# Gate and up products of four feed-forward chunks by seven block products in place of eight, with the weight sums on GpSimd

## The chip, the core and the metric

The kernel runs on one core of one Trainium2 chip. A core has TensorE (PE in the profile) for matrix products, VectorE (DVE), ScalarE (ACT) and GpSimd (POOL) for elementwise work, and SyncE (SP), which here only issues DMAs. Each engine works through its own queue in order and waits on semaphores for the others. Products go to PSUM (eight banks of 128x512 fp32); everything else lies in SBUF. The metric is the device time of one execution in microseconds, the median of three runs.

## The reference

A two-layer network on 256 positions of width 1024, in float32. Each layer is a feed-forward block, a mixer (latent attention and a gated recurrence in layer 0, differential attention in layer 1) and a second feed-forward block, each with a norm before and after and a residual. What matters here is the feed-forward block, which runs four times with weights 1024x2816, 1024x2816 and 2816x1024:

```python
def swiglu(x, w_gate, w_up, w_down):
    return (jax.nn.silu(x @ w_gate) * (x @ w_up)) @ w_down

h = swiglu(rms_norm(x, g[0, 0]), ffn_w_gate[l, 0], ffn_w_up[l, 0], ffn_w_down[l, 0])
x = x + 0.5 * rms_norm(h, g[0, 1])
```

## The kernel before

**Precision.** A product of float32 operands is made of three products of rounded ones: each operand is held as `hi` (rounded to float32r) and `lo` (the rest), and `mm3` adds hi·hi, hi·lo and lo·hi. One k tile of 128 rows and 512 columns is therefore three matmuls. The moving operand is the weight, the stationary one a 128x128 tile of the turned activations.

**Weights.** All weights lie in HBM in one array `w` in the order of use. `emit_load` loads a subunit of [128, 1024] on SP's queue into one of five `raw` buffers (pool `wraw`), ScalarE rounds it (`whi`, line 219), and VectorE subtracts (`wlo`, line 224: SBUF raw less SBUF hi). The pair goes to `queue`; `fill` keeps seven subunits ahead of TensorE. An order on VectorE is forced for all `wlo` (`after`); all other instructions are ordered by a scheduler by their priority, and `high_priority` marks those of norms and turned operands. The `hi` and `lo` of a feed-forward block go to its own pool of `BUFS_F` = 7 pairs, those of other parts to `wsp` with five.

**A feed-forward block.** The 256 positions are two tiles t of 128. The 2816 hidden columns are cut into six chunks, `CHUNKS` = 512, 512, 256, 512, 512, 512. For each chunk `group` makes the gate product of both tiles (`pg`), `silu` reads it, the previous chunk's h is transposed (`turn`, line 353 on TensorE, then a rounding and a split, lines 360 and 361), `group` makes the up product (`pu`), `gated` multiplies (line 445), and `down` adds the previous chunk's part to the four banks y. So each weight subunit is used for both tiles: a gate subunit of two k tiles feeds 2 x 2 x 3 = 12 matmuls, and a down subunit as many. The last two chunks' down products come at the end; there `finish` makes the norm, the residual and the turned operand of the next block, half by half, between the last products. The first chunk is made by `group_first`, tile 0 ahead of tile 1, while tile 1's operand `xT[1]` is still being turned.

**Names.** `xT[t]` is the turned input of a block, (hi, lo), eight k tiles; `hT[t]` the turned h of a chunk; `oT` the turned output of a mixer, free in a feed-forward block. GpSimd makes little: the power -0.5 of each norm (lines 343 and 388), and some elementwise work in the mixers (lines 708, 709, 791, 1007).

Of the kernel before, what the change touches and what calls it, by code (L numbers as in the profile page):

```python
# [12 lines left out]
F32 = mybir.dt.float32  # L13
# [21 lines left out]
BUFS_F = 7  # L35
CHUNKS = [512, 512, 256, 512, 512, 512]

# ---------------------------------------------------------------- weight stream
# A unit is (name, index, first k tile, k tiles, column ranges): [128, k tiles, columns],
# stored contiguously in the order of use.  # L40


def _ffn_units(l, j):
# [12 lines left out]
    for ci, (a, w) in enumerate(starts):  # L56
        step = 2048 // w
        for k in range(0, KD, step):
# [54 lines left out]
for _i in range(1, len(UNITS)):  # L113
    if UNITS[_i - 1][0].endswith("w_out") and not UNITS[_i][0].endswith("w_out"):
# [8 lines left out]
def _pack(inputs):  # L123
    parts = []
    for name, idx, k0, nk, cols in UNITS:
# [6 lines left out]
# ---------------------------------------------------------------- constants of the shapes  # L132
# [37 lines left out]
def forward(ctx, tc, a):  # L170
# [19 lines left out]
    # ------------------------------------------------------------ weight stream  # L190
    SPLIT = 1024
    state = {"i": 0, "off": 0, "block": -1, "pool": None, "first": None, "n": 0}
# [3 lines left out]

    def emit_load():
        if state["i"] >= len(UNITS):
            return
        u = UNITS[state["i"]]  # L200
        pool, tag = (state["pool"], "f") if BLOCK_OF[state["i"]] == state["block"] else (wsp, "w")
# [3 lines left out]
        off = state["off"]  # L205
        state["off"] += P * width
        src = a["w"][off:off + P * width].rearrange("(p n) -> p n", p=P)
        nc_ = width // nk
        per = max(1, SPLIT // nc_)
        for k in range(0, nk, per):  # L210
            n = min(per, nk - k)
            w = n * nc_
            raw = wraw.tile([P, SPLIT], F32, name="raw", tag="raw")
            moved = nc.sync.dma_start(raw[:, :w], src[:, k * nc_:k * nc_ + w])
            if state["n"] in late:
                after(late[state["n"]](), moved)
# [13 lines left out]
    def take(nk):  # L230
        """The next subunits that make up nk k tiles."""
# [31 lines left out]
    def group(pss, lhss, n, nk=KD, k0=0):  # L263
        """pss[t][:, :n] = lhs_t^T @ the next weight group [nk*128, n]; a step of side work after each subunit."""
# [46 lines left out]
    # ------------------------------------------------------------ start  # L311
# [19 lines left out]
    def after(b, a_):  # L331
        """b is issued after a_ (on one engine)."""
# [5 lines left out]
    def rpow(ss, n, mul, add):  # L338
        """(ss * mul + add) ** -0.5"""
# [6 lines left out]
    def to_T(src, dst, n, j0=0, bank=bank):  # L346
        """dst[(hi, lo)][:, j0:j0+n, :] = transposes of the n 128-column blocks of src."""
# [15 lines left out]
    def turn_x(t, xg):  # L363
        """Closures: halves of xT[t] = xg^T, split."""
# [11 lines left out]
    def post_norm(t, ys, g, half, gnext):  # L376
        """x[t] += (0.5 if half) rms(y) g; returns xg = x[t] * gnext."""
# [40 lines left out]
    # ------------------------------------------------------------ FFN  # L418
# [750 lines left out]
```

## Time and profile before

| | |
|---|---|
| Median of three runs | 1028.74 us (1028.34 to 1030.66) |
| Profiled execution, its own span | 1027.8 us |
| TensorE busy | 1011.3 us (98%), 4979 matmuls seen |
| VectorE busy | 625.8 us (61%) |
| ScalarE busy | 517.1 us (50%) |
| GpSimd busy | 49.9 us (5%) |
| HBM read | 182.35 MB, 178 GB/s over the span |

The four feed-forward blocks begin at about 11, 343, 531 and 843 us of the span; the mixers lie from 200 to 340 and from 720 to 840. The profile comes from one execution. Busy times count an instruction from its start to its modelled end; on TensorE instructions overlap, so the distance from one start to the next tells what one costs, not its length.

### The profile page before, as it was taken

What the parts mean: (1) busy time and instruction counts of PE and PEld (TensorE: products, weight loads), DVE (VectorE), ACT (ScalarE), POOL (GpSimd) and SP (SyncE); (2) the same over time, 40 slices, a digit from 0 to 9 for tenths busy, and PEclk for the clock granted to TensorE, in tenths of its full rate; (3) what the DMA queues carried; (4) which work ended last, traced back from release to release, by engine and by line L of the source; (5) the groups of instructions that cost most, each with busy time, mean ns of one, the idle gap of its engine ahead of it and who ended that gap; (6) DMA issues with size and microseconds to landing.
All of it is one profiled execution on the core that took longest, in us unless ns stands there. A gap on an engine that the chain in (4) does not pass through costs nothing.

```text
span 1027.8 us, 13158 instructions
## 1 busy us (share of the span) xinstructions
PE 1011.3 (98%) x4979; PEld 843.5 (82%) x4979; DVE 625.8 (61%) x876; ACT 517.1 (50%) x757; POOL 49.9 (5%) x61
## 2 busy tenths in 40 slices
PE   8999999999999999999999999999999999999997
PEld 6888888888788889888888888888877878888886
DVE  6555585768577855455576555546676786455553
ACT  6544455477644644444554444444665565444441
POOL 1000000021201000000000000000011200000000
PEclk8999999999999999999999999999999999999999
DMA  8765555575221765555547555555634366655531
GB/s 282 271 202 186 186 184 189 180 225 194 86 81 58 253 212 196 185 184 187 182 164 246 187 183 189 191 190 168 208 121 147 102 206 225 201 182 189 186 123 41
DMA packets 51903, 184.25 MB, mean 179 GB/s; under 512 B 6136, under 2 KB 6528, under 8 KB 51840
## 3 DMA queue, kind: packets, MB, share of 16 engines
q1 hardware_dynamic: 48960, 176.05, 51.8%
q10 hardware_dynamic: 2880, 7.37, 2.1%
q8 instruction: 39, 0.64, 0.2%
q14 instruction: 24, 0.20, 0.1%
HBM read 182.35 MB, written 1.05 MB: 178 GB/s over the span
## 4 chain that ended last, share of the span: by engine, by line
PE 90%; DVE 4%; issue 3%; ACT 1%; DMA 1%; POOL 1%; SPq 0%; DVEq 0%; POOLq 0%; ACTq 0%
PE w L244 16%; PE w L246 16%; PE w L245 16%; PE y L246 9%; PE y L244 9%; PE y L245 9%; PE w L292 7%; PE w L353 2%; DVE wlo L224 1%; PE y L353 1%; DMA raw<-in_w_dram 1%; ACT whi L219 1%; POOL pm L1007 0%; DVE E L857 0%; DVE pm L1009 0%
## 5 line engine op out<-in xcount | busy, mean ns | idle before, releaser
L224 DVE TENSOR_TENSOR wlo<-raw,whi 128x1024 fp32r<-128x1024 f32 (+2 forms) x331 | 404.0, 1227 | 283.6 <-ACT whi L219 281.2
L219 ACT CAST whi<-raw 128x1024 fp32r<-128x1024 f32 (+1 forms) x331 | 345.0, 1049 | 365.5 <-PE w L246 206.6
L244 PE MATMUL w<-whi,xThi 128*128 128x512 f32 (+1 forms) x836 | 315.6, 377 | 0.0
L246 PE MATMUL w<-whi,xTlo 128*128 128x512 f32 (+1 forms) x836 | 312.0, 373 | 0.0
L245 PE MATMUL w<-wlo,xThi 128*128 128x512 f32 (+1 forms) x836 | 311.5, 373 | 0.0
L246 PEld LDWEIGHTS w<-whi,xTlo 128*128 128x128 f32 x836 | 157.3, 188 | 28.3 <-issue 0.3
L244 PEld LDWEIGHTS w<-whi,xThi 128*128 128x128 f32 x836 | 157.5, 188 | 27.5 <-issue 1.0
L245 PEld LDWEIGHTS w<-wlo,xThi 128*128 128x128 f32 x836 | 157.5, 188 | 26.4
L244 PE MATMUL y<-whi,hThi 128*128 128x512 f32 x352 | 138.4, 393 | 0.0
L246 PE MATMUL y<-whi,hTlo 128*128 128x512 f32 x352 | 137.2, 390 | 0.0
L245 PE MATMUL y<-wlo,hThi 128*128 128x512 f32 x352 | 137.1, 389 | 0.0
L246 PEld LDWEIGHTS y<-whi,hTlo 128*128 128x128 f32 x352 | 66.1, 188 | 14.0
L245 PEld LDWEIGHTS y<-wlo,hThi 128*128 128x128 f32 x352 | 66.1, 188 | 13.2
L244 PEld LDWEIGHTS y<-whi,hThi 128*128 128x128 f32 x352 | 66.1, 188 | 13.2
L361 DVE TENSOR_TENSOR hTlo<-w,hThi 128x512 fp32r<-128x512 f32 (+1 forms) x48 | 29.1, 640 | 34.0 <-ACT hThi L360 34.0
L440 ACT ACTIVATE s<-w,sm 128x512 f32<-128x512 f32 (+1 forms) x48 | 31.4, 653 | 25.9 <-PE w L246 20.3
L388 POOL TENSOR_TENSOR sm<-sm,mhalf 128x1 f32<-128x1 f32 x12 | 6.6, 550 | 726.6 <-DVE sm L386 726.6
L292 PE MATMUL w<-whi,xThi 128*128 128x512 f32 (+2 forms) x124 | 39.1, 397 | 2.6 <-ACT xThi L360 2.6
L292 PE MATMUL w<-wlo,xThi 128*128 128x512 f32 (+2 forms) x124 | 37.8, 389 | 0.4 <-DVE wlo L224 0.4
L292 PE MATMUL w<-whi,xTlo 128*128 128x512 f32 (+2 forms) x124 | 37.9, 390 | 0.0
L445 DVE SCALAR_TENSOR_TENSOR h<-w,sm,s 128x512 f32<-128x512 f32 (+1 forms) x48 | 32.0, 699 | 0.7 <-PE w L246 0.5
L292 PEld LDWEIGHTS w<-whi,xThi 128*128 128x128 f32 x124 | 22.6, 192 | 6.6 <-ACT xThi L360 3.1
(246 smaller groups left out, 820.2 us busy)
## 6 DMA issues: line engine op xcount, KB each, us to landing
raw<-in_w_dram SPq DMA_DIRECT2D x325, 512.0 KB, 3.6
g<-in_norm_g_dram ACTq DMA_DIRECT2D x9, 512.0 KB, 4.6
raw<-in_w_dram SPq DMA_DIRECT2D x4, 448.0 KB, 3.4
g<-in_norm_g_dram SPq DMA_DIRECT2D x2, 512.0 KB, 6.2
out_dram<-x SPq DMA_DIRECT2D x4, 256.0 KB, 2.1
E<-in_hw_dram ACTq DMA_DIRECT2D x1, 576.0 KB, 6.7
x<-in_x_dram SPq DMA_DIRECT2D x2, 256.0 KB, 3.0
x<-in_x_dram SPq DMA_DIRECT2D x1, 512.0 KB
```

Source lines behind the costliest of these rows:

```text
L219: c = nc.scalar.copy(hi[:, :w], raw[:, :w])
L224: state["lo"] = nc.vector.tensor_tensor(lo[:, :w], raw[:, :w], hi[:, :w].bitcast(F32), op=ALU.subtract)
L244: mm(ps, hi[:, j, :], rhi, start=start, stop=False)
L245: mm(ps, hi[:, j, :], rlo, start=False, stop=False)
L246: state["mm"] = mm(ps, lo[:, j, :], rhi, start=False, stop=stop)
L292: state["mm"] = mm(o, lhs[:, k, :], rhs[:, i, :], start=j == 0 and k == 0, stop=j == 2 and k == KD - 1)
L353: nc.tensor.transpose(ps[:, i * P:(i + 1) * P], src[:, (b + i) * P:(b + i + 1) * P], ident)
L361: return c, nc.vector.tensor_tensor(lo.rearrange("p a b -> p (a b)"), ps, h2.bitcast(F32), op=ALU.subtract)
L388: nc.gpsimd.tensor_tensor(r, v, mhalf[:, :1], op=ALU.pow)
L440: nc.scalar.activation(s[:, :w], ps[:, :w], AF.Silu, scale=r[t])
L445: nc.vector.scalar_tensor_tensor(hh[:, :w], ps[:, :w], r[t], s[:, :w], op0=ALU.mult, op1=ALU.mult)
```

## The change

In the second, fourth, fifth and sixth chunk of each feed-forward block (`SEVEN` counts from 0) gate and up are seen as one product of 2x2 blocks: the rows are the two tiles of positions, the inner dimension is cut into two halves of four k tiles, and the columns are gate (B11 above, B21 below) and up (B12, B22). It is made by seven block products in the form of Strassen and Winograd. Each is [128 x 512] by [512 x 512], four k tiles of three matmuls, for one tile of positions' sum:

- X from A11·B11; W from S1·T1; X adds S2·T2; Y from A12·B21; X adds S3·T3; X adds A22·T4; W adds S4·B22. ScalarE copies X to SBUF three times on the way (`held`), VectorE adds a PSUM bank to a copy three times (`plus`), and `silu` and `gated` read the results.
- Row sums S1 to S4 (`row_sums`, once a block): GpSimd adds hi and lo of `xT`, makes four sums and four `lo`, twelve operations 128x512; ScalarE makes four `hi`. S1 and S2 lie in `oT`.
- Weight sums on GpSimd (`emit_load`), in two tiles of 1024 columns each: T1 = B12 - B11, T2 = B22 - T1, T3 = T2 - B11, T4 = B21 - T2, in place in the raw tiles. T1 to T4 and B11, B21, B22 are each rounded and split as a weight is: 14 subunits a chunk for 8.
- The raw tiles of these chunks come from a pool of eight (`raws`); the pairs of a block come from its own pool, now four, and from `wsp`, five, in turn (`RING`). Of the previous chunk's down products one half stands between T3 and T4, the other behind B22; in the sixth chunk all stand behind.

The core of the diff (comments that the diff removes are left out):

```diff
-BUFS_F = 7
+BUFS_F = 4
+SEVEN = (1,3,4,5)
+RAWS = 8
+RING = "wfwfwfwfw"
...
+        if ci in SEVEN:
+            gate, up = ([("ffn_w_" + n, (l, j), k, 4, [(a, a + w)]) for k in (0, 4)] for n in ("gate", "up"))
...
+            units += [gate[0] + ("B11",), up[0] + ("T1",), up[1] + ("T2",), gate[1] + ("B21",), (None, None, 0, 4, [(a, a + w)], "T3")]
+            units += d[:half] + [(None, None, 0, 4, [(a, a + w)], "T4"), (None, None, 0, 4, [(a, a + w)], "B22")] + d[half:]
+            continue
...
+                raw = (wraw if kind is None else state["raws"]).tile([P, SPLIT], F32, name="raw", tag="raw")
...
+                sub = nc.gpsimd.tensor_tensor
+                if kind in ("B11", "B21"):
+                    kept[kind, k] = raw
+                elif kind == "T1":
+                    sub(raw, raw, kept["B11", k], op=ALU.subtract)
+                    kept["T", k] = raw
+                elif kind == "T2":
+                    kept["B22", k] = raw
+                    sub(kept["T", k], raw, kept["T", k], op=ALU.subtract)
+                    raw = kept["T", k]
+                elif kind == "T3":
+                    raw = kept["B11", k]
+                    sub(raw, kept["T", k], raw, op=ALU.subtract)
+                elif kind == "T4":
+                    raw = kept["B21", k]
+                    sub(raw, raw, kept["T", k], op=ALU.subtract)
+                else:
+                    raw = kept["B22", k]
...
+            def row_sums(fp):
...
+                        tt(A[t][i], hi, lo, op=ALU.add)
+                tt(A[1][1], A[1][0], A[1][1], op=ALU.add)
+                tt(A[1][0], A[0][0], A[1][0], op=ALU.subtract)
+                tt(A[0][0], A[1][1], A[0][0], op=ALU.subtract)
+                tt(A[0][1], A[0][1], A[0][0], op=ALU.subtract)
...
+                    nc.scalar.copy(hi, v)
+                    tt(lo, v, hi.bitcast(F32), op=ALU.subtract)
...
+            def prod(ps, lhs, start):
...
+                        mm3(ps, lhs, k, hi[:, i, :], lo[:, i, :], start and k == 0, k == 3, not start)
...
+                X = bank()
+                prod(X, half(0, 0), True)
+                hT = [turn(0, CHUNKS[ci - 1]), None]
+                W = bank()
+                prod(W, S1, True)
+                p1 = held(X)
+                hT[1] = turn(1, CHUNKS[ci - 1])
+                prod(X, S2, False)
+                Y = bank()
+                prod(Y, half(0, 1), True)
+                u2 = held(X)
+                s0 = silu(0, plus(p1, Y), 512)
+                prod(X, S3, False)
+                downs(range(kf))
+                u3 = held(X)
+                c22 = plus(u3, W)
+                prod(X, half(1, 1), False)
+                s1 = silu(1, X, 512)
+                prod(W, S4, False)
+                h = [gated(0, plus(u2, W), s0, 512), gated(1, c22, s1, 512)]
+                downs(range(kf, wp))
...
+            sums = row_sums(fp)
             for ci in range(1, nch):
                 w, wp = CHUNKS[ci], CHUNKS[ci - 1]
+                if ci in SEVEN:
+                    seven(ci)
+                    continue
...
-    nc = _bacc.Bacc("TRN2", target_bir_lowering=False, num_devices=1)
+    nc = _bacc.Bacc("TRN2", target_bir_lowering=False, num_devices=1, dynamic_dma_scratch_size=512)
```

How this moves instructions, at three places. First VectorE at the start of the third feed-forward block, before: the last splits of the first chunk and of the second chunk's first weights, then the first chunk's h, then on with weights.

```order
L361 TENSOR_TENSOR xTlo1_94<-y_4749,xThi1_93 128x512
...
L224 TENSOR_TENSOR wlo_4803<-raw_4800,whi_4802 128x1024
L224 TENSOR_TENSOR wlo_4809<-raw_4806,whi_4808 128x1024
L445 SCALAR_TENSOR_TENSOR h_4840<-w_4672,sm_4631,s_4729 128x512
L445 SCALAR_TENSOR_TENSOR h_4842<-w_4673,sm_4652,s_4780 128x512
L224 TENSOR_TENSOR wlo_4849<-raw_4846,whi_4848 128x1024
```

The same place after. raw_4965 and raw_4971 are the halves of B11, raw_5010 and raw_5017 hold first T1 and then T2.

```order
L408 TENSOR_TENSOR xTlo1_94<-y_5030,xThi1_93 128x512
L271 TENSOR_TENSOR wlo_4810<-raw_4807,whi_4809 128x1024
L271 TENSOR_TENSOR wlo_4956<-raw_4953,whi_4955 128x1024
L271 TENSOR_TENSOR wlo_4962<-raw_4959,whi_4961 128x1024
L271 TENSOR_TENSOR wlo_4968<-raw_4965,whi_4967 128x1024
L271 TENSOR_TENSOR wlo_4974<-raw_4971,whi_4973 128x1024
L271 TENSOR_TENSOR wlo_5014<-raw_5010,whi_5013 128x1024
L271 TENSOR_TENSOR wlo_5021<-raw_5017,whi_5020 128x1024
L271 TENSOR_TENSOR wlo_5085<-raw_5010,whi_5084 128x1024
L271 TENSOR_TENSOR wlo_5092<-raw_5017,whi_5091 128x1024
L494 SCALAR_TENSOR_TENSOR h_5123<-w_4951,sm_4906,s_5008 128x512
```

Seven splits stand between the operand's last half and the splits of T2 (wlo_5085, wlo_5092), and h now stands behind these two.

Second, GpSimd at the same place, before: only the powers of the norms.

```order
L388 TENSOR_TENSOR sm_4569<-sm_4566,mhalf_87 128x1
L343 TENSOR_TENSOR sm_4631<-sm_4629,mhalf_87 128x1
L388 TENSOR_TENSOR sm_4640<-sm_4637,mhalf_87 128x1
L343 TENSOR_TENSOR sm_4652<-sm_4650,mhalf_87 128x1
```

And after, from the add of tile 1's second half on: xf are the sums, oTlo and Slo the four `lo`, then T2 and T3 of either half.

```order
L524 TENSOR_TENSOR xf_5128<-xThi1_93,xTlo1_94 128x512
L525 TENSOR_TENSOR xf_5128<-xf_5128 128x512
L526 TENSOR_TENSOR xf_5128<-xf_5127,xf_5128 128x512
L527 TENSOR_TENSOR xf_5127<-xf_5128,xf_5127 128x512
L528 TENSOR_TENSOR xf_5127<-xf_5127 128x512
L534 TENSOR_TENSOR oTlo0_96<-xf_5128,oThi0_95 128x512
...
L534 TENSOR_TENSOR Slo1_5140<-xf_5127,Shi1_5139 128x512
L249 TENSOR_TENSOR raw_5010<-raw_5081,raw_5010 128x1024
L253 TENSOR_TENSOR raw_4965<-raw_5010,raw_4965 128x1024
L249 TENSOR_TENSOR raw_5017<-raw_5088,raw_5017 128x1024
L253 TENSOR_TENSOR raw_4971<-raw_5017,raw_4971 128x1024
```

Nine operations stand ahead of T2's first half, and T3's first half stands ahead of T2's second. In the other three blocks T2's halves stand behind the second and the third `lo`.

Third, VectorE around the fifth chunk's h in the second block, before: four splits of 1024 columns since the turned h, then h.

```order
L361 TENSOR_TENSOR hTlo_4095<-w_4096,hThi_4094 128x512
L361 TENSOR_TENSOR hTlo_4104<-w_4105,hThi_4103 128x512
L224 TENSOR_TENSOR wlo_4117<-raw_4114,whi_4116 128x1024
L224 TENSOR_TENSOR wlo_4123<-raw_4120,whi_4122 128x1024
L224 TENSOR_TENSOR wlo_4153<-raw_4150,whi_4152 128x1024
L224 TENSOR_TENSOR wlo_4159<-raw_4156,whi_4158 128x1024
L445 SCALAR_TENSOR_TENSOR h_4186<-w_4112,sm_3141,s_4090 128x512
```

After, the last eight rows ahead of the fifth chunk's h: the sixth chunk's B11, T1 and T2 (raw_4418, raw_4424, raw_4444, raw_4451), with one `plus` (u) between.

```order
L271 TENSOR_TENSOR wlo_4421<-raw_4418,whi_4420 128x1024
L271 TENSOR_TENSOR wlo_4427<-raw_4424,whi_4426 128x1024
L271 TENSOR_TENSOR wlo_4448<-raw_4444,whi_4447 128x1024
L271 TENSOR_TENSOR wlo_4455<-raw_4451,whi_4454 128x1024
L271 TENSOR_TENSOR wlo_4479<-raw_4444,whi_4478 128x1024
L564 TENSOR_TENSOR u_4354<-w_4273,u_4354 128x512
L271 TENSOR_TENSOR wlo_4486<-raw_4451,whi_4485 128x1024
L494 SCALAR_TENSOR_TENSOR h_4471<-u_4354,sm_3282,s_4357 128x512
```

The next chunk's sums and their splits have moved ahead of this chunk's h.

## Rows read from the trace of the kernel before

**Rows 1.** The page: engine, busy us, share of the span, instructions.

```profile
PE 1011.3 (98%) x4979; PEld 843.5 (82%) x4979; DVE 625.8 (61%) x876; ACT 517.1 (50%) x757; POOL 49.9 (5%) x61
```

**Rows 2.** Waits: who waited for whom, total us, times, longest us.

```profile
DVE wlo L224 <- ACT whi L219: 281.2, 227, 2.8
ACT whi L219 <- PE w L246: 206.6, 131, 2.0
```

**Rows 3.** Timeline of TensorE: start us, us, engine, line, operation; twelve matmuls apart.

```profile
389.03 0.39 PE L244 MATMUL y<-whi,hThi 128*128 128x512 f32 x1
...
391.75 0.39 PE L244 MATMUL y<-whi,hThi 128*128 128x512 f32 x1
```

**Rows 4.** Groups by form on VectorE and ScalarE: busy us, mean ns; idle before.

```profile
L224 DVE TENSOR_TENSOR wlo<-raw,whi 128x1024 fp32r<-128x1024 f32 x325 | 398.3, 1231 | 283.6 <-ACT whi L219 281.2
L613 DVE RECIPROCAL lbm<-tmp 128x512 f32<-128x512 f32 x1 | 3.4, 3352 | 0.7 <-ACT tmp L612 0.7
L539 DVE SCALAR_TENSOR_TENSOR ang<-n,ang 128x80 f32<-128x80 f32 x12 | 2.9, 241 | 0.3
...
L219 ACT CAST whi<-raw 128x1024 fp32r<-128x1024 f32 x325 | 340.2, 1053 | 362.0 <-PE w L246 206.6 <-PE y L246 101.9 <-issue 24.5
```

**Rows 5.** Timeline of VectorE in the second feed-forward block.

```profile
407.31 1.22 DVE L224 TENSOR_TENSOR wlo<-raw,whi 128x1024 fp32r<-128x1024 f32 x1 [2.02 <-ACT whi L219]
408.45 1.28 DVE L361 TENSOR_TENSOR hTlo<-w,hThi 128x512 fp32r<-128x512 f32 x2
```

**Rows 6.** Groups by form on GpSimd.

```profile
L708 POOL TENSOR_TENSOR E<-E,lbm 128x512 f32<-128x512 f32 x2 | 2.6, 1290 | 4.8 <-DVE kk L707 4.8
L791 POOL TENSOR_TENSOR pm<-pm,sm 128x1024 f32<-128x1024 f32 x1 | 1.9, 1896 | 6.1 <-DVE sm L790 6.1
...
L791 POOL TENSOR_TENSOR pm<-pm,sm 128x512 f32<-128x512 f32 x1 | 1.0, 1039 | 24.2 <-DVE sm L790 24.2
```

**Rows 7.** Timeline of GpSimd in the mixers.

```profile
234.80 1.37 POOL L709 TENSOR_TENSOR E<-lb,E 128x512 f32<-128x512 f32 x1
...
764.10 1.04 POOL L1007 TENSOR_TENSOR pm<-pm,sm 128x512 f32<-128x512 f32 x1 [7.15 <-DVE rp L570]
770.32 1.97 POOL L1007 TENSOR_TENSOR pm<-pm,sm 128x512 f32<-128x512 f32 x1 [5.18 <-DVE sm L1006]
787.83 1.04 POOL L1007 TENSOR_TENSOR pm<-pm,sm 128x512 f32<-128x512 f32 x1 [15.54 <-PE y L995]
```

**Rows 8.** Timeline of VectorE at the moments of rows 7.

```profile
234.93 2.32 DVE L224 TENSOR_TENSOR wlo<-raw,whi 128x1024 fp32r<-128x1024 f32 x1
...
763.99 0.68 DVE L999 TENSOR_REDUCE sm<-y 128x2 f32<-128x512 f32 x1
...
770.17 1.23 DVE L224 TENSOR_TENSOR wlo<-raw,whi 128x1024 fp32r<-128x1024 f32 x1
...
788.13 1.83 DVE L224 TENSOR_TENSOR wlo<-raw,whi 128x1024 fp32r<-128x1024 f32 x1 [0.47 <-ACT whi L219]
```

**Rows 9.** Timeline of VectorE at the start of the third feed-forward block.

```profile
539.31 0.69 DVE L361 TENSOR_TENSOR xTlo<-y,xThi 128x512 fp32r<-128x512 f32 x1 [2.10 <-ACT xThi L360]
```

**Rows 10.** The chain that ended last, in order of time: start us, us, what.

```profile
13.46 2.53 PE w L292 x6
...
16.43 10.98 PE w L292 x48
...
564.55 0.87 PE w L353 x8
```

More of the change, by code (lines that the diff above doesn't have):

```diff
@@ L113 @@
 for _i in range(1, len(UNITS)):
-    if UNITS[_i - 1][0].endswith("w_out") and not UNITS[_i][0].endswith("w_out"):
+    if (UNITS[_i - 1][0] or "").endswith("w_out") and not (UNITS[_i][0] or "").endswith("w_out"):
         BLOCK_OF[_i - 1] = BLOCK_OF[_i]
@@ L124, in _pack @@
     parts = []
-    for name, idx, k0, nk, cols in UNITS:
+    for name, idx, k0, nk, cols, *_ in UNITS:
+        if name is None:
+            continue
         w = inputs[name][idx][k0 * P:(k0 + nk) * P]
@@ L191, in forward @@
     SPLIT = 1024
-    state = {"i": 0, "off": 0, "block": -1, "pool": None, "first": None, "n": 0}
+    state = {"i": 0, "off": 0, "block": -1, "pool": None, "first": None, "n": 0, "turn": 0}
     queue = []
@@ L195, in forward @@
     late = {}
+    kept = {}
     def emit_load():
@@ L212, in emit_load @@
             w = n * nc_
[L213 to L216, printed above, removed]
+            if u[0] is not None:
+                raw = (wraw if kind is None else state["raws"]).tile([P, SPLIT], F32, name="raw", tag="raw")
+                moved = nc.sync.dma_start(raw[:, :w], src[:, k * nc_:k * nc_ + w])
+                for key in [key for key in late if key <= state["n"]]:
+                    after(late.pop(key)(), moved)
+            if kind is not None:
+                sub = nc.gpsimd.tensor_tensor
[16 more added lines that the diff above has]
+                    raw = kept["B22", k]
+            pool, tag = wsp, "w"
+            if ours:
+                if RING[state["turn"] % len(RING)] == "f":
+                    pool, tag = state["pool"], "f"
+                state["turn"] += 1
             hi = pool.tile([P, SPLIT], F32R, name="whi", tag=tag + "hi")
@@ new lines, in prod, with seven, held, plus @@
+            def prod(ps, lhs, start):
+                k0 = 0
+                while k0 < 4:
+                    fill()
+                    hi, lo, m, _ = queue.pop(0)
+                    for i in range(m):
+                        k = k0 + i
+                        mm3(ps, lhs, k, hi[:, i, :], lo[:, i, :], start and k == 0, k == 3, not start)
+                    k0 += m
+                    pump()
+            def seven(ci):
+                nonlocal h, hT
+                wp = CHUNKS[ci - 1] // P
+                kf = (wp // 2 + 1) // 2 * 2 if ci < nch - 1 else 0
+                wp = wp if ci < nch - 1 else 0
+                S1, S2, S3, S4 = sums
+                def held(ps):
+                    c = fp.tile([P, 512], F32, name="u", tag="u", bufs=2)
+                    nc.scalar.copy(c, ps)
+                    return c
+                def plus(c, ps):
+                    nc.vector.tensor_tensor(c, ps, c, op=ALU.add)
+                    return c
+                def downs(ks):
+                    for k in ks:
+                        sub = take(1)
+                        for t in range(NT):
+                            down(t, sub, 0 if ci == 1 else None, None, k)
+                X = bank()
[19 more added lines that the diff above has]
+                downs(range(kf, wp))
```

38 lines of the change are left out of this document (30 added, 8 removed).

## Prediction

> **What bounds the kernel now.** I read the page's busy shares first: TensorE is busy for 1011.3 of 1027.8 us, VectorE for 625.8, GpSimd for 49.9 [rows 1]. Then the waits: ScalarE's rounding of a weight tile waits mostly for a TensorE matmul (206.6 us in all), and VectorE's split waits for that rounding (281.2 us) [rows 2]. Read backwards: TensorE gives a buffer back, ScalarE and VectorE refill it, and the refill is early. TensorE's own pace bounds the feed-forward blocks. In them twelve 512-column matmuls lie 2.72 us apart, 389.03 to 391.75 [rows 3], so one costs 0.227 us however long its row looks. I call twelve matmuls a unit. The profiled span is 1027.8 us; the median is 1028.74, so 0.9 us lie around it, and I add differences to 1028.7.
>
> **What is removed.** Each changed chunk has 84 gate and up matmuls for 96. That is one unit less, 2.72 us, and 16 chunks (four in each of four blocks) give 43.5 us, 10.9 a block. Nothing on TensorE is added. If the rest stayed hidden, the time would be 985.
>
> **What is added to the other engines.** A changed chunk has 14 split tiles for 8: six more roundings on ScalarE (1.05 us each) and six more splits on VectorE (1.23 us, [rows 4]), besides three sums with a PSUM operand there, and on GpSimd eight subtractions 128x1024. Once a block GpSimd also makes 12 operations 128x512 for the row sums. ScalarE: 18 roundings, 18.9 us, in a chunk of 30.8 us; with copies, silu and turned h some 24, so it is hidden. VectorE alone: 18 splits at 1.14 us from start to start (407.31 to 408.45, [rows 5]) are 20.5 us, and seven operations that read PSUM at about 0.65 us make 25. That would fit too.
>
> The price of GpSimd's 128x1024 with two full operands has no row. With two full operands 128x512 takes 1.29 us; with one operand broadcast 128x1024 takes 1.90 [rows 6]. Bounds are 1.90 and 2 x 1.29 = 2.58; the broadcast rows grow by 0.86 from 512 (1.04) to 1024 columns (1.90), so I take 1.29 + 0.94 = 2.23, a little over that slope. Eight are 17.8 us: GpSimd alone fits as well.
>
> **But the two do not run side by side.** Rows 7 are GpSimd's operations and rows 8 VectorE's at the same moments. At 234.80 GpSimd runs until 236.17; the split that began at 234.93 takes 2.32 us in place of 1.22 and ends 1.08 after it. The split at 788.13 takes 1.83 and ends 1.09 after GpSimd's. The other way, the split at 770.17 keeps its 1.23 and GpSimd's operation at 770.32 takes 1.97 for 1.04, 0.89 of it behind the split's end. So whichever starts first holds something that both need, and the other stands still: a split costs 1.08 behind GpSimd, and GpSimd 0.15 less than its duration behind a split (2.08 for 128x1024). A chunk then needs 18 x 1.11 + 8 x 2.08 = 36.6 us of this shared path, where TensorE needs 30.8 (11 units and 0.9 of transposes).
>
> Whether VectorE's operations with a PSUM operand are stopped too, one row speaks for: the reduction of a PSUM tile at 763.99 keeps 0.68 us beside GpSimd's at 764.10 [rows 7, 8]. I count them half hidden. The Trainium skill (SBUF — State Buffer, section SBUF: two separate sides) says that the pair of ports shared by the two is an exclusive lock for a whole instruction, and that of VectorE's operations those with two SBUF inputs, or in a two-port mode, ask for it. By that rule the PSUM readers are free, as taken here; were they stopped too, 5 us a block would come on top, and the sum below would be 1102. The rows agree with the lock; of sums with one PSUM operand none lies beside GpSimd.
>
> **Start of a block: the row sums.** In the third block, tile 1's last operand is complete at 540.00 [rows 9]. TensorE transposes for the second chunk after its gate group, at 564.55 [rows 10]; 4 units (10.88) before that the first chunk ends, 553.67. After the change the first product follows, 2.72, and then TensorE needs h, at 556.4. But on VectorE h now stands behind the splits of T2, and T2 on GpSimd behind the row sums (the order rows of the change show it). From 540.00: nine GpSimd operations, 11.6; seven splits between them, 7.6; T2, T3, split, T2, T3, split, 4 x 2.08 + 2 x 1.08; h 0.74. That ends at 570.4: TensorE stands for **14.0**. In the other blocks T2 stands two operations earlier and T3 after both: 6 x 1.29 + 6 x 1.08 + 2 x 2.08 + 2 x 1.29 + 3 x 1.08 + 0.74 = 24.9, a wait of **8.5**. With splits already done before 540, or 1.90 for a subtraction, 9.4 and 5; with 2.58, 16 and 11.
>
> **Fourth to sixth chunk: the shared path.** From the third chunk's h, where VectorE is let through, to the sixth chunk's last split there are 44 splits (48.8 us at 1.11), 18 subtractions (37.4) and 16 PSUM readers (10.4, half of it 5.2): 91.4 us. TensorE's work there: 4 units of down, 9, 11 and 7 units and 2.2 of transposes, 86.6. The last split is followed by six matmuls, 1.4. So **6.2** a block are waited for, in the sixth chunk, where no down products lie between. Bounds: 0 (1.75 behind a split, PSUM readers hidden: 80.3) and 19 (2.43, 1.14, nothing hidden: 104.3).
>
> **Smaller terms.** The clock: the first six matmuls of the program take 2.53 us, 0.42 each, the lower level, and the next 48 take 10.98, 0.23 [rows 10]. A wait of 8 to 14 us at a block's start may bring that back; eight matmuls at 0.42 cost 1.6, I take 2 a block (0 to 4). The Trainium skill (TensorE: Matmul & The Clock Gate, Part 1) says that the lower level is the default and activity lifts it. By this rule each long wait is paid again as at the start, and the sum holds; without it, 1073. Before, no wait inside a block is long enough to show it.
> In the second and fourth blocks, behind a mixer, GpSimd's first T1 stands ahead of the norm's power in its queue and waits for a DMA into memory that the mixer gives up: 3 us (0 to 5). The first block has its rotary tables and bounds on VectorE in these chunks: a reciprocal 3.35, twelve 2.9 [rows 4], and some 35 short ones, about 13 in all (0 to 14), formerly hidden; its loads for the second chunk go ahead of three of the first's: 3 (0 to 5); and one T1, 2.1, stands among the row sums.
> Sum: third block -10.9 + 14.0 + 6.2 + 2 = 11.3; second and fourth -10.9 + 8.5 + 6.2 + 2 + 3 = 8.8 each; first -10.9 + 8.5 + 2.1 + 6.2 + 2 + 13 + 3 = 23.9. Together 52.8: **1081.5 us**.
>
> **Rivals.**
> *Side by side, faster.* If the stop in rows 7 and 8 does not hold for in-place subtractions, the fourth to sixth chunks cost nothing, and the starts only GpSimd's own chain: third block 9 x 1.29 + 3 x 2.23 + 1.05 + 1.23 + 0.74 = 21.3, a wait of 4.9; others 1.2. 1028.7 - 43.5 + 4.9 + 3.6 = 994. Against it stand all overlaps that the trace has. Chance 0.08. The same side is reached, near 1015, if the lock holds but all terms lie at their lower ends: 0.08; it decides where a block's waits fall below 10.9.
> *No lead at all, much slower.* If VectorE never gets ahead, each changed chunk takes its full 18 x 1.14 + 8 x 2.08 + 4.5 = 41.7 (33.5 before), 38.8 (28.1) in the fourth and 34.6 (22.6) in the sixth: 39.1 a block, less 13.5 that the third chunk (22.6 of TensorE, 9.1 of splits) gives back. 1028.7 + 4 x 25.6 + 19 = 1150. For it: in-order queues, where a copy waits behind a rounding that waits for GpSimd. Against: nine buffer pairs, and the down products give time. Chance 0.10.
> *Fewer products than said?* Counting the program's matmuls gives 192 fewer; this is no rival.
>
> **How the numbers follow.** The forecast, with waits that outweigh the gain, has 0.70, in 1031 to 1140. Not all bounds meet: low ends together give 1010, high ends 1157. Range 1025 to 1140, with 0.12 left below and 0.08 above. Under 0.2% (about what a measurement here can tell from no change) lie 1026.7 to 1030.8: 0.04. Faster 0.16, slower 0.80.
>
> **What would show it.** Right: splits of about 2.3 us beside subtractions in the changed chunks, a TensorE gap of 8 to 14 us after the first product of each second chunk, gaps in the sixth, fewer in the fifth. Wrong: splits at 1.23 and subtractions at 2.2 us at the same moments; or no gap at the blocks' starts; or gaps through the fourth and fifth chunks, which is the second rival.

## The result, and the profile after

The changed kernel takes 1202.55 us (four runs, 1200.8 to 1206.05) where the kernel before takes 1028.97: a ratio of 1.1685, interval 1.1659 to 1.1712. The forecast was 1081.5 with 1140 as the upper end. The sign is as forecast, the size is not: 173.6 us were lost, not 52.8. The 192 matmuls that are gone should give 43.5, so waits and slow matmuls come to 217 us; the prediction had 96.3.

The page of the changed kernel, its span, busy shares and the chain that ended last, by engine:

```profile
span 1202.0 us, 13377 instructions
...
PE 1021.7 (85%) x4787; PEld 831.9 (69%) x4787; DVE 945.7 (79%) x1020; ACT 635.6 (53%) x917; POOL 511.8 (43%) x237
...
PE 33%; DVE 26%; POOL 17%; issue 14%; ACT 5%; DMA 4%; SPq 0%; ACTq 0%; DVEq 0%; POOLq 0%
```

Against [rows 1], TensorE has fallen from 98% to 85% of a longer span, and GpSimd has risen from 50 to 512 us. On the chain TensorE holds only a third.

The groups of VectorE and GpSimd by line and shape: out<-in, shapes, count, busy us, mean ns of one, idle us before them and what ended it.

```profile
L271 DVE TENSOR_TENSOR wlo<-raw,whi 128x1024 fp32r<-128x1024 f32 x421 | 673.1, 1632 | 151.6 <-ACT whi L266 150.8
L564 DVE TENSOR_TENSOR u<-w,u 128x512 f32<-128x512 f32 x48 | 32.6, 680 | 0.0
L494 DVE SCALAR_TENSOR_TENSOR h<-u,sm,s 128x512 f32<-128x512 f32 x32 | 32.4, 1054 | 0.0
L408 DVE TENSOR_TENSOR hTlo<-w,hThi 128x512 fp32r<-128x512 f32 x40 | 27.0, 682 | 5.7 <-ACT hThi L407 5.7
...
L256 POOL TENSOR_TENSOR raw<-raw 128x1024 f32<-128x1024 f32 x32 | 102.5, 3218 | 46.1 <-DVE wlo L271 37.0 <-ACT hThi L407 6.6 <-ACT whi L266 2.4
```

A split took 1.23 us before and takes 1.63 on average: 421 x 0.40 = 169 us of VectorE standing still. A subtraction on GpSimd takes 2.33 us at its shortest and 2.7 to 3.2 in the means of its four lines.

The table of waits (us in total, times, longest):

```profile
DVE wlo L271 <- ACT whi L266: 153.1, 88, 8.3
...
ACT whi L266 <- POOL raw L249: 123.3, 28, 9.6
PE w L400 <- DVE h L494: 108.4, 13, 17.3
```

In [rows 2] the split's wait for the rounding was 281.2 us of harmless slack, and the rounding waited for TensorE. Now ScalarE waits for GpSimd's T2, and TensorE for VectorE.

TensorE's long waits, from its timeline (start, us, what, and in brackets the idle time before and what ended it), the transposes of h for the second chunk of the four blocks, then for the fifth:

```profile
58.54 1.09 PE L400 MATMUL w<-ident,h 128*128 128x128 f32 x4 [17.30 <-DVE h L494]
...
438.95 1.09 PE L400 MATMUL w<-ident,h 128*128 128x128 f32 x4 [9.99 <-DVE h L494]
...
667.77 1.09 PE L400 MATMUL w<-ident,h 128*128 128x128 f32 x4 [14.14 <-DVE h L494]
...
1011.25 1.09 PE L400 MATMUL w<-ident,h 128*128 128x128 f32 x4 [12.08 <-DVE h L494]
```

```profile
161.87 1.12 PE L400 MATMUL w<-ident,h 128*128 128x128 f32 x4 [8.56 <-DVE h L494]
...
539.38 1.12 PE L400 MATMUL w<-ident,h 128*128 128x128 f32 x4 [10.69 <-DVE h L494]
...
765.11 1.11 PE L400 MATMUL w<-ident,h 128*128 128x128 f32 x4 [11.53 <-DVE h L494]
...
1111.41 1.11 PE L400 MATMUL w<-ident,h 128*128 128x128 f32 x4 [9.08 <-DVE h L494]
```

The gaps at the blocks' starts are there, 10 to 17 us. The second set is what the prediction did not have: it put the starvation into the sixth chunk and "fewer" gaps into the fifth. A shorter wait lies inside the second block's fourth chunk:

```profile
520.23 0.50 PE L291 MATMUL w<-whi,xThi 128*128 128x512 f32 x1 [2.21 <-ACT u L560]
```

By the prediction's own signs, gaps through the fourth and fifth chunks are the mark of its second rival, "no lead at all".

**How the two engines stop each other.** VectorE and GpSimd in the second block, ahead of the wait at 539.38:

```profile
521.94 6.36 DVE L271 TENSOR_TENSOR wlo<-raw,whi 128x1024 fp32r<-128x1024 f32 x2
531.62 3.53 DVE L271 TENSOR_TENSOR wlo<-raw,whi 128x1024 fp32r<-128x1024 f32 x2 [3.32 <-ACT whi L266]
535.07 0.68 DVE L564 TENSOR_TENSOR u<-w,u 128x512 f32<-128x512 f32 x1
535.67 2.98 DVE L271 TENSOR_TENSOR wlo<-raw,whi 128x1024 fp32r<-128x1024 f32 x1
538.58 3.52 DVE L494 SCALAR_TENSOR_TENSOR h<-u,sm,s 128x512 f32<-128x512 f32 x2
```

```profile
521.49 2.40 POOL L249 TENSOR_TENSOR raw<-raw 128x1024 f32<-128x1024 f32 x1 [5.16 <-DVE wlo L271]
523.97 3.25 POOL L253 TENSOR_TENSOR raw<-raw 128x1024 f32<-128x1024 f32 x1
527.18 3.33 POOL L249 TENSOR_TENSOR raw<-raw 128x1024 f32<-128x1024 f32 x1
530.59 2.34 POOL L253 TENSOR_TENSOR raw<-raw 128x1024 f32<-128x1024 f32 x1
535.23 2.35 POOL L256 TENSOR_TENSOR raw<-raw 128x1024 f32<-128x1024 f32 x1 [2.30 <-DVE wlo L271]
```

Two splits need 6.36 us where they would need 2.4, because T2 and T3 run at the same moments; and T3 needs 3.25 where alone (530.59) it needs 2.34. Each waits for the other's end in turn. Adding busy times therefore misleads: VectorE's and GpSimd's sum counts every wait twice. What counts is the time in which at least one of them runs. Worked out from all their rows, that is 20.1 of the 20.2 us from 480.8 to 501.0, 38.3 of 38.4 up to the fifth chunk's transposes and 37.5 of 37.7 up to the sixth's. Without VectorE's operations that read PSUM, which are not stopped (below), it is 20.0, 37.1 and 35.5 us. So the shared path is in use for 94 to 99% of the time in these stages. These sums alone would look much the same if the two engines only waited for each other's results; the run with tiny operations below separates the two.

An operation of VectorE that reads PSUM is not stopped: 15 such operations of lines 564 and 408 (128x512) begin and end inside a subtraction's row and take 0.68 or 0.69 us, no more than elsewhere. Here is one of them at 197.17 (L564), inside GpSimd's subtraction at 196.12; the two h behind it, which read `u` and `s` from SBUF, take 4.99 us together:

```profile
196.12 3.40 POOL L249 TENSOR_TENSOR raw<-raw 128x1024 f32<-128x1024 f32 x1
```

```profile
197.17 0.68 DVE L564 TENSOR_TENSOR u<-w,u 128x512 f32<-128x512 f32 x1
197.88 4.99 DVE L494 SCALAR_TENSOR_TENSOR h<-u,sm,s 128x512 f32<-128x512 f32 x2
```

**The clock.** TensorE behind the wait that ended at 539.38:

```profile
540.72 0.63 PE L292 MATMUL w<-wlo,oThi 128*128 128x512 f32 x1
541.14 0.63 PE L293 MATMUL w<-whi,oTlo 128*128 128x512 f32 x1
...
543.19 0.39 PE L292 MATMUL w<-wlo,oThi 128*128 128x512 f32 x1
543.42 0.40 PE L293 MATMUL w<-whi,oTlo 128*128 128x512 f32 x1
```

The first start 0.42 apart (the level of 1.2 GHz; the granted clock is 0.50 from 540.5 to 543.0), the last 0.23 (2.4 GHz; granted clock 1.00 from 543.2). Over the whole trace 218 matmuls start between 0.33 and 0.6 us after the one ahead, for 21 before; over 0.227 each, that is 42 us more, for 4 before. Of these, 164 start 0.40 or more apart (36.5 us, for 13 and 3.1 before); most of the others are the first matmul behind a short stop, at 0.34. The mean granted clock is 0.939, for 0.996.

### The profile page after: what moved, and what is told of

Same layout as the page of the kernel before. It is cut to its first block, busy times and chain, and to the rows that moved or that the text cites. A ratio compares the mean times of both kernels' runs of the same rounds, so it can differ in the third digit from the quotient of the medians.

```text
span 1202.0 us, 13377 instructions
## 1 busy us (share of the span) xinstructions
PE 1021.7 (85%) x4787; PEld 831.9 (69%) x4787; DVE 945.7 (79%) x1020; ACT 635.6 (53%) x917; POOL 511.8 (43%) x237
## 3 DMA queue, kind: packets, MB, share of 16 engines
HBM read 182.35 MB, written 1.05 MB: 153 GB/s over the span
## 4 chain that ended last, share of the span: by engine, by line
PE 33%; DVE 26%; POOL 17%; issue 14%; ACT 5%; DMA 4%; SPq 0%; ACTq 0%; DVEq 0%; POOLq 0%
DVE wlo L271 17%; PE w L291 5%; POOL raw L249 5%; PE w L292 5%; PE w L293 5%; DMA raw<-in_w_dram 4%; PE y L291 3%; PE y L293 3%; PE y L292 3%; ACT whi L266 3%; PE w L339 3%; POOL raw L253 2%; POOL raw L256 2%; DVE u L564 1%; DVE h L494 1%
## 5 line engine op out<-in xcount | busy, mean ns | idle before, releaser
L271 DVE TENSOR_TENSOR wlo<-raw,whi 128x1024 fp32r<-128x1024 f32 (+1 forms) x427 | 679.1, 1623 | 153.9 <-ACT whi L266 153.1
L266 ACT CAST whi<-raw 128x1024 fp32r<-128x1024 f32 (+1 forms) x427 | 435.0, 1046 | 332.6 <-POOL raw L249 123.3
L291 PE MATMUL w<-whi,xThi 128*128 128x512 f32 (+1 forms) x516 | 193.1, 374 | 26.2 <-DVE hTlo L408 14.1
L292 PE MATMUL w<-wlo,xThi 128*128 128x512 f32 (+1 forms) x516 | 189.5, 367 | 6.0 <-DVE wlo L271 6.0
L293 PE MATMUL w<-whi,xTlo 128*128 128x512 f32 (+1 forms) x516 | 189.3, 367 | 0.0
L245 POOL TENSOR_TENSOR raw<-raw 128x1024 f32<-128x1024 f32 x32 | 92.2, 2891 | 168.8 <-DMA raw<-in_w_dram 142.6
L249 POOL TENSOR_TENSOR raw<-raw 128x1024 f32<-128x1024 f32 x32 | 95.7, 2992 | 142.6 <-DVE wlo L271 142.6
L291 PEld LDWEIGHTS w<-whi,xThi 128*128 128x128 f32 x516 | 98.4, 191 | 48.5 <-ACT u L560 16.5
L400 PE MATMUL w<-ident,h 128*128 128x128 f32 x176 | 32.0, 313 | 108.5 <-DVE h L494 108.4
L256 POOL TENSOR_TENSOR raw<-raw 128x1024 f32<-128x1024 f32 x32 | 102.5, 3218 | 46.1 <-DVE wlo L271 37.0
L292 PEld LDWEIGHTS w<-wlo,xThi 128*128 128x128 f32 x516 | 98.5, 191 | 21.2 <-DVE wlo L271 7.3
L293 PEld LDWEIGHTS w<-whi,xTlo 128*128 128x128 f32 x516 | 98.5, 191 | 16.0 <-issue 0.3
L253 POOL TENSOR_TENSOR raw<-raw 128x1024 f32<-128x1024 f32 x32 | 87.4, 2735 | 2.0
L291 PE MATMUL w<-whi,oThi 128*128 128x512 f32 x128 | 61.0, 477 | 0.1
```

The lines of the kernel that those rows point to most:

```text
L245: sub(raw, raw, kept["B11", k], op=ALU.subtract)
L249: sub(kept["T", k], raw, kept["T", k], op=ALU.subtract)
L253: sub(raw, kept["T", k], raw, op=ALU.subtract)
L256: sub(raw, raw, kept["T", k], op=ALU.subtract)
L266: c = nc.scalar.copy(hi[:, :w], raw[:, :w])
L271: state["lo"] = nc.vector.tensor_tensor(lo[:, :w], raw[:, :w], hi[:, :w].bitcast(F32), op=ALU.subtract)
```

## The experiments

Three theories stood at first. **P**: the path that VectorE's two-operand operations and GpSimd share is full. **B**: the eight raw buffers are one chunk's, so the next chunk's loads wait for this chunk's last sum. **O**: h waits in VectorE's queue behind the next chunk's splits, whatever these cost.

### Without the weight sums

```diff
-                    sub(raw, raw, kept["B11", k], op=ALU.subtract)
... (T2, T3 and T4 likewise)
```

> The eight weight subtractions of each changed chunk are left out (the products take the loaded weights as they are, so the output is another one); products, loads, roundings, splits, row sums and buffers stay. Theory P (the path that GpSimd's and VectorE's two-operand operations share is full in the feed-forward blocks): the path loses 32 x 2.3 = 74 us a block and falls well under TensorE's 177, so only the wait at each block's head for the row sums stays, at most 5 to 10 us a block: 1005 us (990 to 1025). Theory B (eight raw buffers are just one chunk's, so the next chunk's loads wait for this chunk's last use): the loads still wait for the buffers, 1040 to 1100. Theory O (h waits on VectorE behind the next chunk's splits, whatever those cost): the order stays and most of the 108 us of waits for h with it, 1090 to 1150.

Measured: 1041.02 us, ratio 1.0101 (1.0086 to 1.0116). So the 128 weight sums cost 161.5 us, 10.1 in each changed chunk. Above P's range by 16 us, and just inside the lower end of B's (1040 to 1100), so this run doesn't separate these two; the run with tiny operations does. It is far from O's: TensorE's waits for h, one row of the table of waits (us in total, times, longest), fall from 108.4 to

```profile
PE w L395 <- DVE h L489: 28.1, 5, 7.2
```

Four of the five are at the second chunks. Worked out from the starts of TensorE's rows, waits and slow matmuls of the second block compare so (us; each stage ends at the next chunk's first transposes; the first line less what the kernel before has there; in the forecast 8.5 + 3, the clock's 2 and the shared path's 6.2):

| stage of the second block | changed | without weight sums | forecast |
|---|---|---|---|
| up to the second chunk's first transposes | 18.5 | 8.7 | 11.5 |
| from there to the third's | 7.4 | 1.9 | 2 |
| to the fourth's | 0 | 0 | 0 |
| to the fifth's | 13.3 | 0 | 0 |
| to the sixth's | 6.4 | 0 | 0 |
| from there on | 7.4 | 0.2 | 6.2 |

### The weight sums on VectorE

```diff
-                sub = nc.gpsimd.tensor_tensor
+                sub = nc.vector.tensor_tensor
```

> The 32 weight subtractions of each block go from GpSimd to VectorE; nothing else changes. Theory P: each then takes about 1.15 us of the shared path in place of 2.3, 32 x 1.15 = 37 us a block less: 1202 - 4 x 37 = 1054 (1035 to 1080), though VectorE itself has more to do. If GpSimd's help were worth having (no exclusion), it would be slower than 1202 instead, since VectorE's 946 busy us grow by 128 x 1.15 = 147. Theory B: the chain of load, sum, split and release is as long in steps, each sum shorter by 1.1: 1120 to 1160. Theory O: h stands behind still more on VectorE: 1180 or above.

Measured: 1092.79 us (1.0603, 1.0587 to 1.0619). Giving the same work to the busier of the two engines saves 110 us. A sum takes 1.22 to 1.49 us there by the means of its four lines. The time is above P's range too (1035 to 1080): of the changed kernel's 161.5 us, 52 stay. VectorE alone is then full in places, busy for 60.1 of the 60.9 us from 461.9 to 522.8 in the second block; that this makes all of the 52 is not shown.

### h ahead of T2's split

```diff
...
+        if key in t2:
+            after(t2[key], ins)
...
```

(`t2[key]` is the first split of the next chunk's T2, `ins` the chunk's last h.)

> On VectorE, h of each chunk is forced ahead of the split of the next changed chunk's T2, where it stood behind that and, often, T3's; nothing else changes. Theory O: the waits of the transposes for h, 108 us in all, go for the most part: 1110 (1090 to 1135). Theory P: the same path work has to be done before the sixth chunk's products, only in another order; the waits move from h to the splits: 1190 (1175 to 1210). Theory B: as P.

Measured: 1193.85 us (1.1584, 1.1542 to 1.1626). TensorE's waits in this kernel:

```profile
PE w L307 <- ACT u L578: 75.7, 17, 12.1
PE w L307 <- DVE hTlo L424: 19.2, 4, 6.0
PE w L416 <- DVE h L512: 11.0, 4, 6.7
```

The waits for h fell from 108.4 to 11.0, and only 8.7 us were won: 75.7 us of waits for ScalarE's copy `u` (17.2 in the changed kernel) and 19.2 for the split of the turned h stand in their place. Theory O falls. The row on which most waiting is booked named the symptom.

### The buffers alone

```diff
-SEVEN = (1,3,4,5)
+SEVEN = ()
...
-            sums = row_sums(fp)
```

> No chunk is changed and no row sums are made, but the buffers of the changed kernel stay: four pairs in the block's own pool for seven, taken in turn with the other five, and eight raw buffers unused. Theories P and O: VectorE and ScalarE refill early enough, nothing changes: 1029 (1026 to 1032). Theory B in its strong form (the lead was lost with the buffers): 1040 or more.

Measured: 1034.26 us, ratio 1.0037 (1.0024 to 1.0049): the smaller pool costs 4 us by itself, a little more than P allowed and less than B's strong form asks.

### Tiny operations in place of the sums

```diff
-                sub = nc.gpsimd.tensor_tensor
+                def sub(o, p, q):
+                    for _ in range(4):
+                        nc.gpsimd.tensor_tensor(o[:, :1], p[:, :1], q[:, :1], op=ALU.subtract)
```

> Each weight subtraction on GpSimd becomes four dependent subtractions of one column (128x1) on the same tiles, so the output is another one. Four take 4 x 0.55 = 2.2 us, as long as the one they stand for, in the same place of the chain from load to split, but they hardly read or write anything. Theory P (a subtraction costs because VectorE's splits stand still meanwhile): near the kernel without weight sums, 1041: 1050 (1040 to 1070). Theory L (a subtraction costs because the weights come 2.3 us later at each step, with raw buffers for one chunk only): near the changed kernel: 1150 to 1205.

Measured: 1058.48 us (1.0264, 1.0242 to 1.0285). GpSimd's group and VectorE's splits in it:

```profile
L243 POOL TENSOR_TENSOR raw<-raw 128x1 f32<-128x1 f32 x512 | 217.1, 429 | 374.5 <-DVE wlo L273 189.9 <-DMA raw<-in_w_dram 143.7 <-ACT whi L268 4.5
```

```profile
L273 DVE TENSOR_TENSOR wlo<-raw,whi 128x1024 fp32r<-128x1024 f32 x421 | 528.7, 1283 | 169.8 <-ACT whi L268 162.9 <-PE w L295 5.1
```

Four of them take 1.7 us, a little less than the 2.2 that I had expected, and the splits stay at 1.28. So that GpSimd stands in the chain from load to split costs 17.5 us (1058.5 less 1041.0); that its sums are 1024 columns wide costs the other 144. Against an undisturbed subtraction's 2.33 us the four fall short by 0.6; if 1.7 us in the chain cost 17.5, that is an estimated 6 of the 144. This is the run that settles it for the stop and against the latency.

### The products alone

```diff
-                    sub(raw, raw, kept["B11", k], op=ALU.subtract)
... (all four sums)
-                xf = [cp.tile([P, D], F32, name="xf", tag="c") for _ in range(NT)]
... (all of the row sums)
+                return [half(1, 1), half(0, 0), half(1, 0), half(0, 1)]
```

> Weight sums and row sums are both left out (loaded weights and halves of the turned input stand in for them, so the output is another one); products, splits, loads and buffers stay. This is what TensorE gains: 192 matmuls less, 43.5 us. Theory H (what is left at the block heads without weight sums, 1041, comes from the row sums on GpSimd): 985 + 4 for the buffers + up to 10 in the first block = 995 (987 to 1005). If the heads wait for the longer queue of splits alone: 1025 to 1041.

Measured: 999.99 us (0.9705, 0.969 to 0.9719), 30.3 under the kernel before and inside H's range. With the buffers' 4 that is 34 of the 43.5; the rest is waiting, worked out from TensorE's rows as 6 us of gaps and 5 of slow matmuls more than before, most of it in the first block. Row sums cost 1041.0 - 1000.0 = 41.0.

### Raw buffers for two chunks

```diff
-BUFS_F = 4
+BUFS_F = 2
...
-RAWS = 8
-RING = "wfwfwfwfw"
+RAWS = 12
+RING = "wwfwwfw"
...
-                raw = (wraw if kind is None else state["raws"])...
+                raw = (wraw if kind in (None, "B21") else state["raws"])...
```

> Raw buffers for two changed chunks in place of one: twelve in the pool, and the two tiles of B21 in the other raw pool; paid for with two pairs of rounded weights less (seven for nine). Sums, splits and row sums are as they were. Theory P: the shared path has the same work and is as full; 1195 (1180 to 1220). Theory B (the next chunk's loads wait for this chunk's last sum, so nothing can be made ahead): the waits at the heads of the fifth and sixth chunks go, some 20 us a block: 1120 (1090 to 1150).

Measured: 1223.09 us (1.1873, 1.1848 to 1.1899), slower by 20, with two pairs of rounded weights less, and 3 above P's range. B's 1120 is not seen, but the lost pairs may hide a gain: how the 20 divide between gain and loss wasn't tried. What speaks more strongly against B is the run with tiny operations, 1058.48 with the raw buffers as they were.

### Two chunks on GpSimd

```diff
-SEVEN = (1,3,4,5)
+SEVEN = (3,5)
```

> Only the fourth and sixth chunks are changed, the second and fifth stay as before; sums on GpSimd. TensorE gains 8 units, 21.8 us. Theory P: the path then has about 78 x 1.1 + 16 x 2.3 + 15.5 + 30 = 168 us of work a block, under TensorE's 183, and the unchanged chunk ahead of each changed one lets VectorE get ahead: 1028.7 - 21.8 + 4 (buffers) + 0 to 20 = 1020 (1011 to 1031). If each changed chunk simply costs the same 10 us that it costs in the changed kernel (161 us in 16 chunks): 1028.7 - 21.8 + 4 + 80 = 1091.

Measured: 1076.14 us (1.0442, 1.0416 to 1.0468). Neither fits. I had left out of the expectation what a block's start costs. There, in the second block, VectorE ahead of the first chunk's h, and GpSimd with the row sums:

```profile
388.97 11.02 DVE L271 TENSOR_TENSOR wlo<-raw,whi 128x1024 fp32r<-128x1024 f32 x5 [2.80 <-ACT whi L266]
399.90 0.74 DVE L494 SCALAR_TENSOR_TENSOR h<-w,sm,s 128x512 f32<-128x512 f32 x1
```

```profile
389.91 2.29 POOL L528 TENSOR_TENSOR xf<-xf 128x512 f32<-128x512 f32 x1
392.16 2.28 POOL L534 TENSOR_TENSOR Slo<-xf,Shi 128x512 fp32r<-128x512 f32 x1
394.40 2.27 POOL L534 TENSOR_TENSOR oTlo<-xf,oThi 128x512 fp32r<-128x512 f32 x1
```

Each row sum of 1.30 us becomes 2.28, and each split 2.2: the two engines go strictly by turns.

### Sums on VectorE, fewer chunks

Row sums are on VectorE too now and made only ahead of the fourth chunk; `SEVEN` is (3,4,5), (3,5), (3,4) or (4,).

```diff
-                tt = nc.gpsimd.tensor_tensor
+                tt = nc.vector.tensor_tensor
...
-            sums = row_sums(fp)
...
+                    if ci == SEVEN[0]:
+                        sums = row_sums(fp)
```

> Three chunks changed (fourth, fifth, sixth), all sums on VectorE, the row sums made only ahead of the fourth chunk. TensorE gains 12 units, 32.6 us. Theory P: VectorE has about 84 x 1.14 + 24 x 1.15 + 12 x 0.65 + 35 = 166 us of work a block against TensorE's 180, and no row sums stand at the block heads: 1028.7 - 32.6 + 4 (buffers) + 4 x 3 = 1012 (1000 to 1030). If consecutive changed chunks cost by themselves, whoever makes the sums: above 1040.

> As the one before with two chunks, fourth and sixth: the kernel with two chunks on GpSimd (1076), with all its sums on VectorE and the row sums later. TensorE gains 21.8 us. Theory P: 78 x 1.14 + 16 x 1.15 + 8 + 33 = 148 us of VectorE work a block against 183: 1028.7 - 21.8 + 4 + 0 to 8 = 1014 (1009 to 1022). If two changed chunks cost 17 us a block for reasons other than the shared path (1076 over 1007, by four): 1065 to 1080.

> Two chunks, fourth and fifth, sums on VectorE: the sixth, which has no down products to give VectorE time, stays as before. Theory P: as for fourth and sixth or a little better, since the last split of the sixth is not waited for: 1013 (1008 to 1022). If neighbouring changed chunks are the cause: 1025 or more.

> One chunk, the fifth, sums on VectorE. TensorE gains 10.9 us. Theory P: 1028.7 - 10.9 + 4 + 0 to 4 = 1023 (1020 to 1027).

| changed chunks | us | ratio and interval |
|---|---|---|
| fourth, fifth, sixth | 1055.39 | 1.025 (1.0218 to 1.0281) |
| fourth and sixth | 1020.34 | 0.9909 (0.9893 to 0.9926) |
| fourth and fifth | 1034.59 | 1.0045 (1.003 to 1.006) |
| fifth | 1027.43 | 0.9981 (0.997 to 0.9992) |

Only fourth and sixth lies in P's range. The fifth alone is 0.4 above it, and the two kernels with neighbouring changed chunks lie where the rival beside P, that neighbours cost, had put them. Fourth and sixth beat both kernels, by 9.4 us against the runs of before beside them. Its page:

```profile
span 1016.0 us, 13231 instructions
...
PE 994.4 (98%) x4883; PEld 824.6 (81%) x4883; DVE 787.9 (78%) x1060; ACT 584.6 (58%) x845; POOL 52.3 (5%) x61
```

TensorE is at 98% again, as in [rows 1]. Neighbours cost: my block sums, 148 and 166 us of VectorE's work, were averages again. By themselves 18 splits at 1.14, 8 sums at 1.15, three `u` at 0.68 and two h at 0.74 are 33 us for TensorE's 31, without the turned h; an unchanged chunk in between pays that off, a changed one doesn't. That fits the order of the four. The 14 us between fourth-and-sixth and fourth-and-fifth are TensorE's: its idle time is 27.8 us for 15.7 and its slow starts cost 8.0 for 5.5, and 7.0 of the idle time are waits of the transposes for h, at most 1.8 each. That VectorE's shortfall in the second neighbour makes all of it is argued, not shown.

### Where the 56 us went

> Fourth and sixth chunks changed, weight sums on GpSimd, row sums late and on VectorE: between the kernel that has both on GpSimd (1076) and the one that has both on VectorE (1020). If the row sums at the blocks' heads make the 56 us between them (they cost 41 us where there were no weight sums): 1030 (1022 to 1040). If the weight sums make them, although the chunk ahead of each changed one gives VectorE time: 1060 (1050 to 1072).

> The changed kernel with the row sums alone moved to VectorE, at the same place; weight sums stay on GpSimd. If the path is full from a block's start to its sixth chunk, the time falls by what the row sums take of it, 12 x (1.29 - 0.65) = 8 us a block, and by what they cost behind one another on GpSimd: 1165 (1150 to 1180). If row sums and weight sums hide each other (the heads wait for T2 either way): 1195 or more.

The first is the kernel with fourth and sixth chunk, with only `sub` back on GpSimd: 1047.24 us (1.0173, 1.0144 to 1.0201), between the two expectations. Of the 56 us, the row sums at the start make 29 (1076.1 to 1047.2) and the weight sums in spaced chunks 27 (to 1020.3), 3.4 a changed chunk for being on GpSimd and not on VectorE; the same difference in the changed kernel is 110 us, 6.9 a chunk. The second is the changed kernel with only `tt` on VectorE: 1176.32 us (1.1407, 1.1386 to 1.1428), 26 less than the changed kernel; near the 1165 of a full path and not 1195.

> The kernel with two changed chunks on VectorE, with the buffers dealt out anew: six raw buffers for the changed chunks, B21 in the other raw pool, and the room to one more pair of rounded weights (ten in all). The smaller pool cost 4 us where nothing else was changed; a part of it comes back: 1018 (1015 to 1021).

Measured: 1028.3 us over ten runs that spread from 1026.16 to 1036.21 (0.9981, 0.9961 to 1.0001): worse than with the buffers as they were, and above the expected 1021. Six raw buffers leave no slack over what one chunk holds (two each of B11, B12 and B22); that this is the cause was not tried. Why it spreads so is open.

## Why the prediction was wrong

**The step that failed** is the term for the shared path, "6.2 a block", 25 us in all. Without the weight sums the kernel takes 161.5 us less, 40.4 a block; by the run with tiny operations up to 144 of these are the stop.

- *The mechanism was right.* A split behind GpSimd takes 2.3 to 3.4 us, and only operations with two SBUF operands are stopped. The Trainium skill (SBUF — State Buffer, section SBUF: two separate sides) has the rule of the exclusive lock; the trace agrees, with 0.68 or 0.69 us for all 15 PSUM readers that run inside a subtraction's row. They were free; the prediction says "free, as taken here", but its sum has them half stopped. Free, they take 5.2 a block off it, 1061 in all, further from what was measured. I had counted h of the changed chunks among them; it reads SBUF there and rose from 0.74 to 1.05 in the mean, six of the 32 to 2.2 to 2.9.
- *The price of one chunk was nearly right.* I had 36.6 us of shared path for TensorE's 30.8. A split behind a subtraction ends 1.08 after it, as forecast. Behind a split a subtraction takes 2.26 us of the path, not 2.08; the split here ends at 514.07, the subtraction at 516.33:

```profile
510.65 3.43 DVE L271 TENSOR_TENSOR wlo<-raw,whi 128x1024 fp32r<-128x1024 f32 x1
```

```profile
512.95 3.37 POOL L245 TENSOR_TENSOR raw<-raw 128x1024 f32<-128x1024 f32 x1
```

  That is 8 x 0.18 = 1.4 a chunk more, 38.1.
- *The way from the chunk to the block was wrong.* I let VectorE be level with TensorE at the third chunk's h, and asked only that it be done by the sixth chunk's last split. From 487.7, when that h is made in the second block, 44 splits and 20 subtractions lie ahead (forecast: 44 and 18). At the trace's prices, with the PSUM readers free, my sum still gives only 44 x 1.11 + 20 x 2.26 + 1.4 - 86.6 = 8.8. In the trace the last of these splits ends at 592.1, 104.4 us after that h, as much as my upper bound of 104.3:

```profile
590.85 1.22 DVE L271 TENSOR_TENSOR wlo<-raw,whi 128x1024 fp32r<-128x1024 f32 x1
```

  And TensorE doesn't wait once at the end: 33 matmuls of the sixth chunk's products are still to come then, where I had six. It has waited before, at the fifth and the sixth chunk's transpositions for an h that stands in the same full queue, then for `u`, and each long wait leaves slow matmuls behind. From the fourth chunk's transposes on that is 13.3 + 6.4 + 7.4 = 27.1 us in the table above, for my 6.2. The second chunk, to which I had given the clock's 2 alone, cost 7.4. How much of this is the fuller path and how much the waiting at each chunk, no run separates.
- *The two dear cases add.* I had "no lead at all" (1150, chance 0.10) as a rival to the forecast's waits at the heads. It was the nearest, and it isn't an alternative to them: 1150 + 14.0 + 3 x 8.5 + 4 x 2 = 1197.5, beside 1202.5 measured. This sum was made afterwards; that the kernel pays just these terms is not shown.

**The heads**: 14.0 in the third block, measured 14.14. For the others I had 8.5, and 3 more in the second and fourth; the rows have 9.99, 12.08, and 17.30 in the first, where I had 2.1 more for T1. So the waits at the transposes came out as forecast or a little longer, but the whole way to them costs 18.5 in the second block for my 11.5: TensorE waits in the first chunk already, 3.36 us for a split at 405.52. Row sums alone cost 41.0 where there are no weight sums; my 14.0 + 25.5 were 39.5, but with T2 and T3 in them, so that these two agree is in part luck. No run separates the first block's 13 + 3; without any sums that block has 6 us more of idle time and slow starts than before.

**The clock**: 2 a block; the slow starts cost 38 us more, 9.5 a block, 33 of them at 0.40 or more, since there were far more waits. The Trainium skill (TensorE: Matmul & The Clock Gate, Part 1) has activity lift the lower level; in the trace each of the eight waits for h listed above is indeed paid again, with four to eleven starts of 0.40 us or more among the next twenty.

**TensorE's gain**: 43.5; 30.3 of it came through without any sums, the buffers' 4 and some waiting of the six added splits aside. Buffers I had at nothing.

**The range** ended at 1140: the case above it had a chance of 0.10 and was joined with nothing. The changed kernel by the runs: 1030.2 (before, beside them) + 4.1 buffers - 34.3 products and their splits + 41.0 row sums + 17.5 for GpSimd in the chain + 144.0 for what its sums hold = 1202.5. Each term is the difference of two runs, so the sum closes by itself; it says what each step costs in this order.

## What to carry to other kernels

Before work goes to GpSimd, add up the time in which either it or VectorE runs two-operand work on SBUF, and compare it with the bound engine's time chunk by chunk, not over a block: here one path was full and the same sums on VectorE were 110 us cheaper. Where the added work fits on average only, put unchanged work between the changed pieces. And when one wait dominates the table, remove that wait alone before believing it: 97 us of waits for h went away, and 9 us of the time.

## What the runs showed of the hardware

I had not expected that strict turns would be so common: beside row sums of 1.30 us, every split and every row sum takes 2.2 to 2.3 for several in a row, and beside 1024-column sums both often take 3.3 to 3.4. Turns are not a rule, though: two of the 128 subtractions stand still through three splits in a row, here 5.57 us long:

```profile
578.91 5.57 POOL L256 TENSOR_TENSOR raw<-raw 128x1024 f32<-128x1024 f32 x1 [3.62 <-DVE wlo L271]
```

```profile
578.75 3.48 DVE L271 TENSOR_TENSOR wlo<-raw,whi 128x1024 fp32r<-128x1024 f32 x3
```

A GpSimd operation of one column (0.43 us) leaves the splits at 1.28. And slow starts of matmuls, which I had as a footnote, made 38 of the 217 us, 33 of them at 0.40 us or more.
